# Moving the activations by 64 and 256 bytes in a two-layer encoder's MLPs, with the gates' weights and the sums of x handled at other places

## The chip, the cores and the metric

The kernel runs on one core of one Trainium2 chip. The metric is device time in microseconds (us) for one execution; three runs of a kernel give a median. A profile is one more execution, taken by the hardware profiler. Engines are named as the profile names them: PE is TensorE (PEld its weight loads), DVE is VectorE, ACT is ScalarE, POOL is GpSimd, SP is SyncE, which only issues DMAs here.

## What is computed

Two layers on x of 512 rows by 1024 features, all float32: layer 0 mixes by stick-breaking attention, layer 1 by a gated linear recurrence (RG-LRU), and each is followed by an MLP of squared ReLU with 4096 inner features.

```python
for layer in range(2):
    h = rms_norm(x, norm_mix[layer])
    x = x + (stick_breaking_attention(h, ...) if layer == 0 else rglru_block(h, ...))
    h = rms_norm(x, norm_mlp[layer])
    u = relu(h @ w1[layer]);  x = x + (u * u) @ w2[layer]
return rms_norm(x, norm_final)

# rglru_block: proj = h @ w_in; gate = gelu(proj[:, :1024]); xc = conv4(proj[:, 1024:])
# r, i = sigmoid of two block-diagonal products of xc (16 blocks of 64x64: "the gates' weights")
# log_a = -8 r softplus(-lam); hs = scan(a, sqrt(1 - a^2) * i * xc); y = (hs * gate) @ w_o
```

## The kernel before

**Numbers in two halves.** Every float32 product is made of three matmuls in the type fp32r: an operand is split into a high half (a cast, on ACT) and a low half (value minus high half, on DVE), and high x high, low x high and high x low are added in PSUM. Activations lie feature by row: `xgh` and `xgl` are the halves of x times the norm's weight, 8 chunks of 128 features by 512 rows, 2048 bytes of a partition for each chunk. `bh` and `bl` are a second pair of the same size. Weights come as 512 KB blocks by DMA (`raw`, or `b`), are split into `wh` and `wl`, and are used once. So for each block ACT casts for about 1.05 us and DVE subtracts for about 1.2 us.

**Order.** PE's instructions stand as the code writes them. The other engines' are placed by a scheduler at build time, except where the code chains them (`Ordered`). Each engine runs its own list in order and waits on semaphores.

**The MLP.** The first quarter of the inner features ("the squares", `squared`, lines 222 to 224 in the profile) is 8 dense products of 24 matmuls with 512 columns of x as the moving operand and a 128x128 weight tile as the stationary one. After it, products of two by two blocks are made by a scheme with seven products instead of eight (`PRODUCTS`: P1 to P7), which works on halves of rows and of features. There are four "down" stages of 14 parts (`times`, line 1067: the moving operand is `wh` or `wl`, 512 columns; the stationary one is the activation in `bh`, `bl`, `sh`, `sl`), and three "up" stages between them of 14 units (`up`, line 972: the moving operand is an activation, 256 columns, 24 matmuls a unit). An up stage runs P1, P5, P6, P3, P7, P2, P4 twice. What each reads as the moving operand is in `xa`: P1, P2 and P4 read `xgh` and `xgl` alone; P7 reads `xgh` and, for the low half, `low`; P3 and P5 read `s41` and `low`; P6 reads `s2` (in `bh` and `bl`) and `low`. P1 and P7 read chunks 0 to 3, P2 and P4 chunks 4 to 7.

**Sums of x.** `s41`, `s2`, `s3` and `low` hold halves of sums of chunks k and k+4 of x (`sums_of_x`: two ACT scalings, four DVE sums; `halves_of_sums`: three casts and three subtractions). They are needed from the first up stage on. k = 0 and 1 are done in the squares, k = 2 and 3 in the first down stage, at its places 19 and 20, 24 and 25; `replace` at place 26 puts `s3` over part of `xgh`. Place 14 is the first part of that stage, 27 its last.

**The gated recurrence.** Its steps on ACT, DVE and POOL follow a string, `ORDER`: `R` fetches raw gates' weights for four chunks, `W` and `X` make their halves, `f`, `a`, `x` fetch and split a weight block (`z0` is a block of the gate, `c2` of the conv's input), `P` is a product on PE, `N`, `r` the norm, `G` the gates' matmuls. The string begins with

```python
R0 fz0 fz1 fc3 Pc2 fc4 W1 W0 X1 X0 az0 xz0 N fc5 Pz0 az1 r ac3 jc3 W2 ac4 xz1 n0 fz2 n1 Pz1 b0 b1
```

`gate_raw` takes a tile `graw` of its own and fetches it on SP's queue (line 1405). In the product c2, after four of its eight chunks, PE makes the norm's sum (line 1470), which needs the squares of all eight chunks added up in `ssq` (line 159).

**Places in memory.** What lies where in a partition follows from the order in which tiles are made. In the built program `xgh`, `xgl`, `bh`, `bl`, `sh`, `sl` and the weights' `raw`, `wh`, `wl` begin at multiples of 128 bytes; all tiles of the attention, `low`, and `s41` begin 64 bytes past one. Chunks, halves and slices are whole multiples of 512 bytes, so an operand's place within 128 bytes is that of its tile. Two more weight buffers in the recurrence (pool `wmore`) lie 64 bytes past.

Of the kernel before, what the change touches and what calls it, by code (L numbers as in the profile page):

```python
# [11 lines left out]
F32 = mybir.dt.float32  # L12
F32R = mybir.dt.float32r
# [4 lines left out]
P = 128  # L18
S = 512
D = 1024  # L20
C = D // P
DFF = 4096
H = 16
HD = 64
EPS = 1e-6
RG_C = 8.0
SCALE = HD ** -0.5
ASIDE = 16


START = [
# [15 lines left out]


ORDER = """
R0 fz0 fz1 fc3 Pc2 fc4 W1 W0 X1 X0 az0 xz0 N fc5 Pz0 az1 r ac3 jc3 W2 ac4 xz1 n0 fz2 n1 Pz1 b0 b1  # L50
t0 ac5 jc4 n2 h0 X2 b2 l0 fc6 az2 t2 G0 jz2 Pc3 t1 s0 W3 h2 X3 h1 z1 R4 fz3 ac6 l1 l2 G1 n3 xc6 G2
s1 z0 Pc4 xc5 b3 s2 m0 fc7 fz4 fz5 m2 t3 E0 az3 T0 jz3 d0 Pc5 h3 E1 n4 ac7 m1 l3 T1 az4 d1 b4 E2
T2 G3 n5 jz4 d2 Pz2 fz6 xc7 q2 q0 t4 fz7 q1 s3 k0 W4 Pc6 h4 m3 b5 fo0 l4 W6 z2 k1 E3 g2 Pz3 n6 T3
# [9 lines left out]
def hybrid_encoder(  # L63
# [23 lines left out]
    nc = tc.nc  # L87
    V, A, G, PE = nc.vector, nc.scalar, nc.gpsimd, nc.tensor
# [15 lines left out]
    def f(ap):  # L104
        return ap.bitcast(F32)
# [11 lines left out]
    make_identity(nc, ident)  # L117
    eps_t = const.tile([P, 1], F32, tag="eps", name="eps_t")
    V.memset(eps_t, EPS)
    ss = const.tile([P, S // P, 3], F32, tag="ss", name="ss")  # L120
    bias = const.tile([P, S // P], F32, tag="bias", name="bias")

    xgh = const.tile([P, C, S], F32R, tag="xgh", name="xgh")
    xgl = const.tile([P, C, S], F32R, tag="xgl", name="xgl")
    bh = const.tile([P, C, S], F32R, tag="bh", name="bh")
    bl = const.tile([P, C, S], F32R, tag="bl", name="bl")

# [16 lines left out]
    class Squares:  # L144


        def __init__(self):
            self.acc = work.tile([P, S], F32, tag="ssq", name="ssq", bufs=1)
            self.begun = False
# [132 lines left out]
    NB = S // P  # L282
# [10 lines left out]
    with ExitStack() as actx:  # L293
# [238 lines left out]
        class Spread:  # L532
# [6 lines left out]
            def __getitem__(self, at):  # L539
                k = at[1] - self.k0  # L540
                return self.tiles[k // 4][:, k % 4, :]
# [198 lines left out]
    def residual(srcs, gname, begun={}, ready={}):  # L740

        for c in range(C):
            add_x(c, begun[c][0] if c in begun else dense(srcs[c], bh, bl, halves=ready.get(c)))
            halves(gname, c, x[c])

    residual(w_so, "mlp0", so, so_next)


    NQ = DFF // D
    HS = S // 2  # L750
# [21 lines left out]
    class Mlp:  # L772
# [170 lines left out]
        def replace(self):  # L943

            for i, t in enumerate(self.s3):
                self.A.copy(xgh[:, 2 * i : 2 * i + 2, HS:], f(t).rearrange("p (k n) -> p k n", k=2))

        def slots_of(self, p):

# [154 lines left out]
        def run(self, first, between, end):  # L1104
# [13 lines left out]
            def place(i):  # L1118

                return (i + self.STEPS // 2) % self.STEPS  # L1120
# [71 lines left out]
            def leave(i):  # L1192
# [6 lines left out]
                if kind == "down":  # L1199
                    if p:  # L1200
                        for n in range(2):
                            self.collect(name, n, bank[n])
                    prepare(ahead)
                    if q4 == 0:

                        k = {19: 2, 20: 2, 24: 3, 25: 3}.get(place(i))
                        if k:
                            (self.sums_of_x if place(i) in (19, 24) else self.halves_of_sums)(k)
                        if place(i) == 26:
                            self.replace()  # L1210
                    return
                u, three = us[p], bank.rearrange("p (i n) -> p i n", i=2)
# [85 lines left out]
        def quarters(self, between, end):  # L1298
            for c in range(C - 1):
                self.squared(c)  # L1300
                p, i = c // 4, c % 4 // 2
                if c % 2:
                    self.split(p, i, slice(0, 3), slice(0, 3))
                    self.sums(p, i)
                    self.split(p, i, slice(0, 4), slice(3, 7))
                if c == 0:
                    units = self.from_down(0)
                    self.load(units, *self.FROM_UP)
                if c < 2:

                    for n in range(4 * c, 4 * c + 4):
                        self.sq.chunk(n, x[n], e=V)
                if c == C - 2:
                    self.rr = self.sq.inv_squares(self.bank())
                between(c)

                k = c - 4
                if k in (0, 1):
                    with tc.issue_after(self.squares.ins):
                        self.sums_of_x(k)  # L1320
                        self.halves_of_sums(k)
            self.run(units, between, end)
            self.blocks.close()

    with ExitStack() as mctx:
# [16 lines left out]
            last["low"] = halves("mix1", c, x[c])  # L1342

        def end(ws, xs):
            for i in range(2):
                for g in range(2):
                    mlp.times("P4", g, i, ws[g], xs[i], False)
                mlp.collect("P4", i, xs[i])
                if i == 0:
                    for c in range(4, C):  # L1350
                        feature(c, "zzoo"[c - 4])
                        squares.chunk(c, x[c], e=G)
# [36 lines left out]
    with ExitStack() as rctx:  # L1389
# [11 lines left out]
        graw = {}  # L1401

        def gate_raw(c0):
            t = rp1.tile([P, 4, 2, HD], F32, tag="graw", name="graw")
            nc.sync.dma_start(out=t, in_=w_gate[:, c0 : c0 + 4])
            for c in range(4):
                graw[c0 + c] = t[:, c]

# [177 lines left out]
        for k in range(C):  # L1586
            for c in range(4):
                ps, wh, wl = begun[c]
                three(ps, bh[:, k, :], bl[:, k, :], wh[:, k, :], wl[:, k, :], k == 0, k == C - 1)

    residual(w_ro, "mlp1", begun, {4: ws["o4"]})
    wctx.close()


    with ExitStack() as mctx:
# [24 lines left out]


        A.activation(mlp.c[0][:, 0, :1], eps_t, AF.Sqrt)

        EV, EA = Ordered(V), Ordered(A)

# [152 lines left out]
```

## Time and profile before

| | |
|---|---|
| median of 3 runs | 1040.48 us (1039.40 to 1040.63) |
| profiled execution | 1040.69 us, of which the span from first to last instruction is 1039.0 us |
| PE, PEld | busy 1028.2 us (99%), 900.5 us (87%) |
| DVE, ACT, POOL | busy 863.4 us (83%), 702.2 us (68%), 167.0 us (16%) |
| granted TensorE clock | 0.998 of full speed over the span |
| HBM | 137.41 MB read, 136 GB/s over the span |

How to read what follows: a line of the chain of waits has start, length, engine, tile, source line and count. Matmuls overlap each other in the records (a matmul's own time is longer than the distance to the next), so the pace of PE is read from the chain's lengths, which go from start to start, or from two starts in the timeline. In the timeline a bracket gives the idle time before an instruction and what ended it.

### The profile page before, as it was taken

Reading aid. Unit: us, or ns where it says so; the run is one execution under the profiler, and the core shown is the slowest. Engines: PE = TensorE matmul, PEld = TensorE weight load, DVE = VectorE, ACT = ScalarE, POOL = GpSimd, SP = SyncE. Lnnn points to the kernel's source line nnn. Section 1 sums busy time; section 2 is a strip of 40 time slices with the busy share of each in tenths; the row PEclk is TensorE's granted clock in tenths of the full one; section 3 lists DMA queues with packets and bytes.
Section 4 is the critical chain, followed back from the end, with each engine's and each line's share of the span. In section 5 each row is a group of like instructions: output and inputs, shape, how many; then the busy total and the mean of one; then the engine's idle time right before and its main releaser. Section 6 shows DMA issues by size and latency. Waiting matters only on the chain.

```text
span 1039.0 us, 15867 instructions
## 1 busy us (share of the span) xinstructions
PE 1028.2 (99%) x5868; PEld 900.5 (87%) x5868; DVE 863.4 (83%) x1152; ACT 702.2 (68%) x1082; POOL 167.0 (16%) x233
## 2 busy tenths in 40 slices
PE   9999999999999999999999999999999999999997
PEld 7888888888888988988988788888888988988986
DVE  7888787848788898898899799984789798898897
ACT  6777676826766773774775699964755773863866
POOL 0444344420010010010011111100000010010012
PEclk9999999999999999999999999999999999999999
DMA  7745454528546667667682484352436667667663
GB/s 233 218 119 144 121 147 102 163 88 300 136 82 188 189 136 205 167 139 205 163 212 80 115 198 120 97 221 86 98 74 175 168 151 195 169 146 195 156 128 108
DMA packets 52829, 159.41 MB, mean 153 GB/s; under 512 B 6673, under 2 KB 7953, under 8 KB 52753
## 3 DMA queue, kind: packets, MB, share of 16 engines
q1 hardware_dynamic: 41664, 119.87, 35.3%
q0 software_dynamic: 10368, 37.75, 21.9%
q8 instruction: 46, 0.75, 0.3%
q10 hardware_dynamic: 720, 0.79, 0.2%
q14 instruction: 31, 0.25, 0.1%
HBM read 137.41 MB, written 4.19 MB: 136 GB/s over the span
## 4 chain that ended last, share of the span: by engine, by line
PE 87%; DVE 7%; issue 2%; ACT 2%; DMA 1%; DVEq 0%; SPq 0%; ACTq 0%; POOL 0%; POOLq 0%
PE ps_t L1067 13%; PE ps_acc L972 8%; PE ps_z L972 7%; PE ps_acc L1067 7%; PE ps_acc L222 5%; PE ps_acc L223 5%; PE ps_acc L224 5%; PE ps_o L972 4%; PE ps_z L1067 3%; DVE wl L762 2%; PE ps_t L223 2%; PE ps_t L224 2%; PE ps_t L222 2%; PE ps_o L222 2%; PE ps_o L223 2%; PE ps_o L224 2%
## 5 line engine op out<-in xcount | busy, mean ns | idle before, releaser
L762 ACT CAST wh<-b 128x1024 fp32r<-128x1024 f32 x168 | 174.4, 1051 | 124.9 <-DVE b L762 77.4
L762 DVE TENSOR_TENSOR wl<-b,wh 128x1024 fp32r<-128x1024 f32 x168 | 203.7, 1220 | 48.1 <-ACT wh L762 47.8
L1049 POOL DMA_DIRECT2D b<-in_w_dn x40 | 35.0, 875 | 357.9 <-DVE b L762 202.0
L222 PE MATMUL ps_acc<-xgh,wh 128*128 128x512 f32 x192 | 78.5, 409 | 0.0
L217 DVE TENSOR_TENSOR wl<-raw,wh 128x512 fp32r<-128x512 f32 (+2 forms) x70 | 62.1, 912 | 15.9 <-ACT wh L215 15.8
L223 PE MATMUL ps_acc<-xgh,wl 128*128 128x512 f32 x192 | 75.2, 392 | 0.0
L224 PE MATMUL ps_acc<-xgl,wh 128*128 128x512 f32 x192 | 75.1, 391 | 0.0
L586 DVE TENSOR_TENSOR_SCAN scan<-keep,later 128x128 f32<-128x128 f32 (+1 forms) x64 | 59.4, 931 | 17.1 <-ACT keep L576 10.5
L762 ACT ACTIVATE u<-u 128x512 f32<-128x512 f32 x100 | 63.1, 632 | 6.0 <-DVE u L762 4.3
L215 ACT CAST wh<-raw 128x512 fp32r<-128x512 f32 (+2 forms) x70 | 50.6, 759 | 23.0 <-PE ps_acc L224 7.3
L590 POOL TENSOR_TENSOR w<-w,scan 128x128 f32<-128x128 f32 (+1 forms) x64 | 51.4, 805 | 56.3 <-DVE scan L586 53.3
L762 DVE TENSOR_TENSOR b<-b,b 128x1024 f32<-128x1024 f32 x48 | 58.7, 1223 | 1.3
L1049 POOL DMA_DIRECT2D b<-in_w_up x24 | 20.8, 868 | 239.7 <-DVE b L762 71.7
L762 DVE TENSOR_TENSOR u<-u 128x512 f32<-128x512 f32 (+1 forms) x92 | 54.9, 596 | 2.7 <-ACT u L762 1.1
L972 PE MATMUL ps_z<-xgh,wh 128*128 128x256 f32 x192 | 54.3, 283 | 0.0
L972 PE MATMUL ps_z<-xgh,wl 128*128 128x256 f32 x192 | 54.1, 282 | 0.0
L762 ACT CAST wh<-raw 128x1024 fp32r<-128x1024 f32 x46 | 48.0, 1047 | 9.1 <-PE ps_acc L1067 8.3
L972 PE MATMUL ps_acc<-low,wh 128*128 128x256 f32 x192 | 53.5, 279 | 0.0
L1067 PE MATMUL ps_t<-wl,sh 128*128 128x512 f32 x126 | 49.2, 390 | 0.3 <-DVE wl L762 0.3
L1067 PE MATMUL ps_t<-wh,bh 128*128 128x512 f32 x126 | 49.2, 390 | 0.0
L1067 PE MATMUL ps_t<-wl,bh 128*128 128x512 f32 x126 | 49.1, 390 | 0.0
L1067 PE MATMUL ps_t<-wh,sl 128*128 128x512 f32 x126 | 49.1, 389 | 0.0
(398 smaller groups left out, 3416.0 us busy)
## 6 DMA issues: line engine op xcount, KB each, us to landing
b<-in_w_dn SPq DMA_DIRECT2D x48, 512.0 KB, 4.6
b<-in_w_dn POOLq DMA_DIRECT2D x40, 512.0 KB, 5.7
b<-in_w_up SPq DMA_DIRECT2D x36, 512.0 KB, 4.6
b<-in_w_up POOLq DMA_DIRECT2D x24, 512.0 KB, 5.5
raw<-in_w_m SPq DMA_DIRECT2D x16, 512.0 KB, 4.2
raw<-in_w_dn SPq DMA_DIRECT2D x16, 512.0 KB, 4.6
raw<-in_w_in SPq DMA_DIRECT2D x16, 512.0 KB, 4.3
raw<-in_w_qk SPq DMA_DIRECT2D x12, 512.0 KB, 3.8
```

The lines of the kernel that those rows point to most:

```text
L215: A.copy(wh[:, k, :], raw[:, k, :])
L217: V.tensor_tensor(wl[:, k, :], raw[:, k, :], f(wh[:, k, :]), ALU.subtract)
L222: PE.matmul(ps, wh, ah, start=start, stop=False)
L223: PE.matmul(ps, wl, ah, start=False, stop=False)
L224: PE.matmul(ps, wh, al, start=False, stop=stop)
L586: V.tensor_tensor_scan(sc[:, S - n : S][:, ::-1], keep[:, :n][:, ::-1], later[:, S - n :][:, ::-1], 1.0, ALU.mult, ALU.max,)
L590: G.tensor_tensor(wt, wt, sc[:, S - n + 1 : S + 1], ALU.mult)
L762: ins = getattr(self.e, name)(*args, **kwargs)
L972: PE.matmul(ps[:, i * HS : (i + 1) * HS], m, y, start=new and i == k == n == 0, stop=i == 1 and k == C // 2 - 1 and n == 2, skip_group_che ...
L1049: G.dma_start(out=unit[b].rearrange("p j n -> p (j n)"), in_=unit["src"](to), accum_op=ALU.add)
L1067: PE.matmul(ps, m, y[:, jj, cols], start=first and n == 0, stop=last and n == 2, skip_group_check=not new,)
```

## The change

Four things are edited.

- **Where x lies.** `xgh` and `xgl` become two views of one tile `x_t`, with 256 bytes (`FRONT`, 64 elements) left free ahead of the first and 512 ahead of the second. A call `x_down` sets how far down (towards lower addresses) the first chunk and the others lie: 256 and 64 bytes from each residual ahead of an MLP to the MLP's last products, and nothing elsewhere. `replace` now copies chunk by chunk (four copies of 128x256 for two of twice the size), since a view gives one chunk at a time.
- **Gates' weights.** `graw` takes the work pool's tile `sq` and is fetched on POOL's queue; in `ORDER` the splitting of z0 and z1 stands ahead of the gates' weights.
- **Sums of x.** In layer 1, k = 2 is done in the squares as well, k = 3 at places 19 and 20, and `replace` at place 21. Layer 0 keeps its places.
- **Small tiles.** `ss` and `bias`, used at the very end, move into columns of `colt` that are free by then.

```diff
-ASIDE = 16
+ASIDE, FRONT = 16, 64
 ORDER = """
-R0 fz0 fz1 fc3 Pc2 fc4 W1 W0 X1 X0 az0 xz0 N fc5 Pz0 az1 r ac3 jc3 W2 ac4 xz1 n0 fz2 n1 Pz1 b0 b1
+R0 fz0 fz1 fc3 Pc2 fc4 az0 xz0 az1 xz1 W1 W0 X1 X0 N fc5 Pz0 r ac3 jc3 W2 ac4 n0 fz2 n1 Pz1 b0 b1
...
-    ss = const.tile([P, S // P, 3], F32, tag="ss", name="ss")
-    bias = const.tile([P, S // P], F32, tag="bias", name="bias")
-    xgh = const.tile([P, C, S], F32R, tag="xgh", name="xgh")
-    xgl = const.tile([P, C, S], F32R, tag="xgl", name="xgl")
+    x_t = const.tile([P, 2 * C * S + 3 * FRONT], F32R, tag="xg", name="xg")
+    class Chunks:
+        def __init__(self, i):
+            self.start, self.down = FRONT + i * (C * S + 2 * FRONT), (0, 0)
+        def __getitem__(self, at):
+            p, c, cols = at
+            a = self.start + c * S - self.down[c > 0]
+            return x_t[p, a : a + S][:, cols]
+    xgh, xgl = Chunks(0), Chunks(1)
+    def x_down(*down):
+        xgh.down = xgl.down = down
...
+    x_down(FRONT, ASIDE)
     residual(w_so, "mlp0", so, so_next)
...
-                self.A.copy(xgh[:, 2 * i : 2 * i + 2, HS:], f(t).rearrange("p (k n) -> p k n", k=2))
+                for j in range(2):
+                    self.A.copy(xgh[:, 2 * i + j, HS:], f(t)[:, j * HS : (j + 1) * HS])
...
-                        k = {19: 2, 20: 2, 24: 3, 25: 3}.get(place(i))
+                        k = ({19: 2, 20: 2, 24: 3, 25: 3}, {19: 3, 20: 3})[self.layer].get(place(i))
...
-                        if place(i) == 26:
+                        if place(i) == 26 - 5 * self.layer:
                             self.replace()
...
-                if k in (0, 1):
+                if k in range(2 + self.layer):
...
         def end(ws, xs):
+            x_down(0, 0)
...
-            t = rp1.tile([P, 4, 2, HD], F32, tag="graw", name="graw")
-            nc.sync.dma_start(out=t, in_=w_gate[:, c0 : c0 + 4])
+            t = work.tile([P, S], F32, tag="sq", name="graw")
+            t = t.rearrange("p (c i n) -> p c i n", c=4, i=2)
+            G.dma_start(out=t, in_=w_gate[:, c0 : c0 + 4])
...
+    x_down(FRONT, ASIDE)
     residual(w_ro, "mlp1", begun, {4: ws["o4"]})
...
+        free = colt[:, COLS["conv"][0] :]
+        ss = free[:, : 3 * NB].rearrange("p (t i) -> p t i", i=3)
+        bias = free[:, 3 * NB : 4 * NB]
```

**Places after.** With `ss` and `bias` gone and 768 bytes added, every later tile moves by 672 bytes. Weights, `bh`, `bl`, `sh` and `sl` now begin 32 bytes past a multiple of 128, and the attention's tiles, `low` and `s41` begin 96 past. x lies 32 past outside the MLPs; in them its first chunk lies 32 past and the others 96 past. So the distances within 128 bytes between any two operands are what they were, but for chunks 1 to 7 of x in the MLPs. PE's list is the same instructions in the same order.

**DVE at the start of the recurrence, before**, from the last subtraction for `xgl` on (`wl` on line 217 is block c2, the two on line 762 are z0 and z1; line numbers in the second piece are those of the changed kernel, 14 to 15 higher here):

```order
L133 SCALAR_TENSOR_TENSOR xgl<-x,colt,xgh 128x512 x3
L217 TENSOR_TENSOR wl<-raw,wh 128x1024
L159 TENSOR_TENSOR ssq<-ssq,sq 128x512 x4
L762 TENSOR_TENSOR gl<-graw,gh 64x2x64 x4
L762 TENSOR_TENSOR wl<-raw,wh 128x1024
L762 RECIPROCAL r<-r 128x512
L762 TENSOR_TENSOR wl<-raw,wh 128x1024
L762 TENSOR_TENSOR ps_acc<-ps_acc,r 128x512 x2
```

and in the changed kernel:

```order
L147 SCALAR_TENSOR_TENSOR xg<-x,colt,xg 128x512 x3
L231 TENSOR_TENSOR wl<-raw,wh 128x1024
L173 TENSOR_TENSOR ssq<-ssq,sq 128x512
L777 TENSOR_TENSOR wl<-raw,wh 128x1024 x2
L173 TENSOR_TENSOR ssq<-ssq,sq 128x512 x3
L777 TENSOR_TENSOR gl<-graw,gh 64x2x64 x4
L777 RECIPROCAL r<-r 128x512
L777 TENSOR_TENSOR ps_acc<-ps_acc,r 128x512 x2
```

z0's and z1's low halves moved ahead of the gates' weights and of three of the four additions to `ssq`. ACT's casts for z0 and z1 moved in the same way, in among the last castings of x.

**DVE at the end of layer 1's squares, before**, from the reciprocal of the row norms on (`u` and `x` with 256 columns are sums of inner activations and of x):

```order
L176 RECIPROCAL rr<-rr 128x4
L762 TENSOR_TENSOR low<-x,s_7350 128x512
L762 TENSOR_TENSOR u<-u 128x256
L177 TENSOR_SCALAR rr<-rr 128x4
L762 TENSOR_TENSOR u<-u 128x256 x2
L762 TENSOR_TENSOR sl<-u,sh 128x1024
L762 TENSOR_TENSOR sl<-u,sh 128x768
L762 TENSOR_TENSOR wl<-b_7421,wh 128x1024
```

and in the changed kernel, from the second of the four sums for k = 2 on:

```order
L777 TENSOR_TENSOR x<-x 128x256
L777 TENSOR_TENSOR u<-u 128x256
L777 TENSOR_TENSOR x<-x 128x256
L777 TENSOR_TENSOR low<-x,s_7735 128x256
L777 TENSOR_TENSOR x<-x 128x256
L777 TENSOR_TENSOR sl<-u,sh 128x1024
L777 TENSOR_TENSOR low<-x,bl 128x256
L777 TENSOR_TENSOR low<-x,s_7349 128x512
L777 TENSOR_TENSOR sl<-u,sh 128x768
L777 TENSOR_TENSOR wl<-b_7420,wh 128x1024
```

The four sums and three subtractions for k = 2 moved here, ahead of `sl` and of the first `wl` of the down stage, from the middle of that stage.

## The prediction

> **What bounds the kernel now.** I read the page first: span, busy times, and the shares of the chain that ended last.
>
> ```profile
> span 1039.0 us, 15867 instructions
> PE 1028.2 (99%) x5868; PEld 900.5 (87%) x5868; DVE 863.4 (83%) x1152; ACT 702.2 (68%) x1082; POOL 167.0 (16%) x233
> PE 87%; DVE 7%; issue 2%; ACT 2%; DMA 1%; DVEq 0%; SPq 0%; ACTq 0%; POOL 0%; POOLq 0%
> ```
>
> PE is the bound. So there are two ways to gain: the pace of its matmuls, and the few places where it waits. The waits of PE, by who ended them:
>
> ```profile
> PE ps_t L223 <- DVE wl L762: 0.8, 1, 0.8
> PE ps_z L972 <- ACT u L762: 0.6, 1, 0.6
> PE ps_acc L972 <- ACT u L762: 0.4, 1, 0.4
> PE ps_t L1067 <- DVE wl L762: 0.3, 1, 0.3
> ```
>
> These four are what the edits outside the addresses can touch: the first stands at the start of the recurrence, the others in layer 1's first stages. For the pace I read the chain in time order through the second half of an up stage of layer 0. Its rows are P1, P5, P6, P3, P7, P2, P4 in this order, 24 matmuls each. The last row is 24 matmuls of a down stage, with 512 columns.
>
> ```profile
> 349.41 2.88 PE ps_z L972 x24
> 352.29 2.74 PE ps_o L972 x24
> 355.03 2.83 PE ps_z L972 x24
> 357.85 2.72 PE ps_o L972 x24
> 360.57 2.83 PE ps_z L972 x24
> 363.40 2.86 PE ps_o L972 x24
> 366.26 2.88 PE ps_z L972 x24
> ...
> 310.64 5.44 PE ps_acc L1067 x24
> ```
>
> The same 24 instructions of the same size take 2.72 us in P3 (113.3 ns each) and 2.88 us in P4 (120 ns). What differs is where the moving operand lies. P3 and P5 read `s41` and `low`, 64 bytes past a multiple of 128, while the weights begin at such a multiple. P1, P2 and P4 read x, which lies at the same place within 128 bytes as the weights. P6 and P7 read one tile of either kind, and take 2.83. So with 256 columns, operands at distance 64 go at 113.3 ns and operands at distance 0 at 120. I take this as a rule of this trace, since it holds in all seven products.
>
> The Trainium skill says otherwise (SBUF — State Buffer, the section on its two separate sides): PE has its own ports and never waits on another engine there, and weight loads have a second, independent read port; by that the place would not matter. The rows above disagree, 2.72 against 2.88 us, so I follow them.
>
> **Term A, the up stages.** The change puts chunks 1 to 7 of x at distance 64, as `s41` is now. Per unit of seven: P1 goes from 2.88 to 2.72, P2 from 2.86, P4 from 2.88, P7 from 2.83, and P5 loses the 0.02 in which it recovers from P1: 0.16 + 0.14 + 0.16 + 0.11 + 0.02 = 0.59 us. P6 reads `s2`, which doesn't move. But the first chunk lies at distance 0 still, in 6 of P1's 24 matmuls and in 4 of P7's. At 6.7 ns each that is 0.04 and 0.03, and each return from it costs about the 0.02 seen in P5, twice in P1 and perhaps once in P7. I take 0.12 off and use 0.47. There are 2 such halves in each of 3 stages in 2 layers, so 12 x 0.47 = 5.6 us. The best is 12 x 0.59 = 7.1; if the first chunk spoils P1 and P7 whole, P2, P4 and 0.02 are left, 12 x 0.32 = 3.8.
>
> **Term B, the squares.** These read x with 512 columns, and there the trace doesn't show distance 64 of this sign. At distance 0 a matmul takes 5.44 / 24 = 226.7 ns. The nearest row with distance 64, of the other sign (weights of pool `wmore` 64 past, x at 0), is product z1, whose first matmul and first successor are
>
> ```profile
> 589.73 0.39 PE L222 MATMUL ps_o<-xgh,wh 128*128 128x512 f32 x1
> 595.22 0.39 PE L1519 MATMUL ps_z<-bh,gh 128*128 128x512 f32 x1
> ```
>
> so 24 take 5.49 us, 228.8 ns each: with 512 columns distance 64 is the worse place, by 2.1 ns. Of each product of the squares 21 matmuls change; 16 products x 21 x 2.1 ns = 0.7 us, and I take a loss of 0.8. It might be nothing, or the full 6.7 ns of the narrow matmuls, 2.25 us.
>
> **Term C, the start of the recurrence.** The rows of SP's queue, ACT, DVE and PE:
>
> ```profile
> SPq L1405 <- DVE ssq L159: 2.3, 1, 2.3
> 576.90 0.33 SPq L1405 DMA_DIRECT2D graw<-in_w_gate  x1
> 580.75 1.26 ACT L762 CAST gh<-graw 64x128 fp32r<-64x128 f32 x4 [8.13 <-DMA graw<-in_w_gate]
> 582.04 1.05 ACT L762 CAST wh<-raw 128x1024 fp32r<-128x1024 f32 x1
> 573.94 2.94 DVE L159 TENSOR_TENSOR ssq<-ssq,sq 128x512 f32<-128x512 f32 x4
> 583.12 1.23 DVE L762 TENSOR_TENSOR wl<-raw,wh 128x1024 fp32r<-128x1024 f32 x1 [0.75 <-ACT wh L762]
> 579.40 1.02 PE L1470 MATMUL ps_z<-ssq,ones 128*128 128x512 f32 x2
> 582.79 0.39 PE L224 MATMUL ps_t<-xgl,wh 128*128 128x512 f32 x1
> 584.41 0.50 PE L223 MATMUL ps_t<-xgh,wl 128*128 128x512 f32 x1 [0.76 <-DVE wl L762]
> ```
>
> The gates' weights are fetched late, since their tile is free only after `ssq`; ACT idles 8.13 us for them, and z0's cast and subtraction stand behind. PE's second matmul of z0 was due two paces after 582.79, at 583.25, and started at 584.41, 1.16 late; with the restart I count 1.2 us. After the change z0 and z1 are split first: that wait goes. What is late next is the norm's sum on PE (L1470), which needs `ssq` complete. DVE begins these additions at 573.94 now and ends at 576.88; with two subtractions of about 1.2 us put in among them it ends near 579.3, and PE wants it at 579.40. ACT's two casts of 1.05 us also come in among the last castings of x, and may hold DVE up by as much as 1 us. So the new wait is 0 to 0.9 us; I take 0.4, and the gain is 0.8, with bounds of 0.3 and 1.2. Nothing else hides behind it: PE's order is the same, and the gates' own weights, now on POOL's queue and no longer behind `ssq`, are wanted only after z0 and z1 (first gates' matmul at 595.22).
>
> **Term D, the sums of x in layer 1.** Layer 0 and layer 1 run the same PE list here. I compare their first two down and up stages, start to start:
>
> ```profile
> 291.23 2.72 PE ps_t L1067 x12
> 446.71 2.75 PE ps_t L1067 x12
> ...
> 758.36 0.39 PE L1067 MATMUL ps_t<-wh,bh 128*128 128x512 f32 x1
> 916.87 2.75 PE ps_t L1067 x12
> ```
>
> Layer 0 takes 155.48 us and layer 1 takes 158.51: 3.0 us are lost to the waits listed above and to the restarts after them. They come late in the first down stage's work of DVE: there ACT waits for DVE (`wh` of `b`), and POOL's next DMA for DVE's `wl`. What one pair of chunks costs DVE is half of these rows, taken over the stretch with k = 2 and k = 3 (776 to 803 us):
>
> ```profile
> L762 DVE TENSOR_TENSOR x<-x 128x256 f32<-128x256 f32 x8 | 3.4, 423 | 0.2
> L762 DVE TENSOR_TENSOR low<-x,s 128x512 fp32r<-128x512 f32 x2 | 1.4, 692 | 0.2
> L762 DVE TENSOR_TENSOR low<-x,bl 128x256 fp32r<-128x256 f32 x2 | 0.8, 418 | 0.0
> L762 DVE TENSOR_TENSOR low<-x,s 128x256 fp32r<-128x256 f32 x2 | 0.8, 418 | 0.0
> ```
>
> (3.4 + 1.4 + 0.8 + 0.8) / 2 = 3.2 us leave the stretch ahead of the waits and go to the end of the squares, where DVE idles:
>
> ```profile
> 757.19 1.23 DVE L762 TENSOR_TENSOR sl<-u,sh 128x1024 fp32r<-128x1024 f32 x1 [1.11 <-ACT sh L762]
> 760.72 0.96 DVE L762 TENSOR_TENSOR sl<-u,sh 128x768 fp32r<-128x768 f32 x1 [2.31 <-ACT sh L762]
> 766.93 0.50 PE L1067 MATMUL ps_z<-wl,bh 128*128 128x512 f32 x1
> ```
>
> 1.11 + 2.31 = 3.4 us of idle time takes nearly all of it, but not quite: 2.1 us stand ahead of the first `sl` and delay the sums of u that ACT's `sh` waits for. By the rows the second `sl` comes 0 to 0.9 us later, and PE, which waits a little for DVE at 766.93 already, waits as much more. I take 0.65. So DVE is 3.2 - 0.65 = 2.5 us ahead where PE used to wait, and this stretch ends 2.5 us earlier: not 3.0 plus the two halves of term A in it, since DVE becomes the limit again. As 2 x 0.47 = 0.94 stand in term A, D is 1.6. It could be 2.0 with all 3.2 us gained, or -0.9 if DVE's work is only late at another place and PE can't use A's part there either.
>
> **Edits at no cost.** `replace` in four copies is ACT work and ACT is busy 68%; if its cover fails it is 0.4 us. `ss` and `bias` in `colt` leave ACT's and DVE's last instructions as they were.
>
> **The sum.** 5.6 - 0.8 + 0.8 + 1.6 = 7.2 us off the profiled execution's 1040.69 gives 1033.5. That execution lies 0.21 above the median of the runs, so against the runs it is 1033.3; I give 1033.4. Two runs of this kernel can be told apart from about 0.2%, 2 us.
>
> **The rivals.**
>
> *Everything works.* All terms at their best: 7.1 + 0 + 1.2 + 2.0 = 10.3 us, 1030.4. It needs the first chunk to cost nothing, for which no row speaks. Chance 0.15.
>
> *The squares pay and DVE is only late elsewhere.* B at 2.25, D at -0.9: 5.6 - 2.25 + 0.8 - 0.9 = 3.2, 1037.5. For it speaks that from 760.72 on DVE shows no idle time; against it, the 3.4 us of idle time just ahead. Chance 0.15.
>
> *The place doesn't matter.* If the difference between the products came from something else in them, A and B are 0, C is 0.8 and D its full 2.5: 3.3 us, 1037.4. By the Trainium skill's page named above (SBUF — State Buffer) this is what one would forecast. P1 to P7 have the same instruction and the same weights' buffers, and split exactly by tile, so I give it 0.06.
>
> *Slower: the shift of everything by 32 bytes.* All operands of PE lay at multiples of 64 bytes and now lie 32 past one. If such a start costs a matmul what distance 64 costs with 512 columns, 2.1 ns, then 5868 x 2.1 ns = 12.3 us are lost, and A and B vanish: 1040.7 + 12.3 - 3.3 = 1049.7. It decides from 7.2 us / 5868 = 1.2 ns a matmul on. One moving operand of the attention lies so now, `lastl`, beside `tl`, which lies at 64:
>
> ```profile
> L635 PE MATMUL ps_o<-lastl,v 128*128 128x256 f32 x16 | 4.6, 287 | 0.0
> L635 PE MATMUL ps_o<-tl,v 128*128 128x256 f32 x16 | 4.5, 282 | 0.0
> ```
>
> 287 against 282 ns in the records' own lengths: little speaks for it, but weights at such a place are not shown at all. Chance 0.12.
>
> **Chances and range.** The forecast itself, 1031.5 to 1035.5, has 0.52. The range 1030.3 to 1037.6 takes in the bounds of the terms and all cases but the slower one. Faster by more than 0.2%: 0.52 + 0.15 + 0.15 + 0.06, less a little for mixtures, 0.86; slower 0.12; within 0.2% 0.02.
>
> **What would show it.** In the changed profile's chain, rows of 24 at P2 and P4 with 2.72 (term A right) or 2.86 to 2.88 (wrong), P1 and P7 near 2.78; the squares' products of 24 near 5.49; no wait of PE for z0's `wl`, and perhaps one ahead of the norm's sum; layer 1's first two down and up stages in about 154 us. The prediction is wrong if P3 and P5 leave 2.72 or down-stage rows leave 5.44, which is the shift by 32 bytes; if P2 and P4 stay; or if PE waits more than 2 us in layer 1's first down stage.

## The result, and the profile after

The changed kernel takes 1037.43 us (median; 1036.74 to 1038.42), the kernel before, on the same chip, 1040.51 us. The ratio is 0.9973, with a 95% interval of 0.9962 to 0.9983. So it is faster, but by 3.1 us where 7.1 were forecast. The profiled execution took 1038.42 us.

The page of the changed kernel: span, busy times and the chain that ended last.

```profile
span 1036.7 us, 15868 instructions
PE 1026.0 (99%) x5868; PEld 893.5 (86%) x5868; DVE 861.0 (83%) x1152; ACT 702.5 (68%) x1086; POOL 174.2 (17%) x235
PE 78%; DVE 12%; ACT 6%; issue 3%; DMA 1%; SPq 0%; DVEq 0%; ACTq 0%
```

Before, 87% of the chain was PE and 7% DVE. Now DVE and ACT hold 18% of it together: in some stretches PE is no longer what ends last. The waits of PE say where (lines have moved: `down` is now L1083, `up` L988, the dense products L236 to L238, the helper L777):

```profile
PE ps_acc L443 <- ACT xg L146: 1.4, 2, 1.0
PE ps_t L1083 <- DVE wl L777: 1.2, 5, 0.3
PE ps_z L399 <- DVE eps_t L119: 1.1, 1, 1.1
PE ps_o L236 <- DVE x L752: 0.2, 1, 0.2
```

The waits at z0 and in layer 1's first stages are gone. New are five waits in the down stages, one behind an up stage each. The profile puts only 1.2 us on them, but they cost more: at the first one it lists 0.26 us, but against the kernel before PE loses 0.55 us there, and 0.35 us more a little earlier in the same stage, in small delays where no wait is listed. In the chain by order of time, the end of the first up stage and the down stage behind it:

```profile
345.26 2.72 PE ps_z L988 x24
347.98 2.72 PE ps_acc L988 x24
350.70 2.76 PE ps_z L988 x24
353.46 2.72 PE ps_o L988 x24
...
382.24 1.32 DVE c L777 x2
383.56 1.14 DVE b L777
...
384.78 1.06 ACT wh L777
...
385.87 1.24 DVE wl L777
...
387.15 2.79 PE ps_t L1083 x11
389.94 5.44 PE ps_acc L1083 x24
```

The first four rows are P2, P4, P1 and P5: 2.72, 2.72, 2.76 and 2.72, where 2.86, 2.88, 2.88 and 2.74 stood before. Then the chain leaves PE: a sum of weights on DVE (`b`), its cast on ACT, its subtraction on DVE, and PE starts 0.04 us after that.

To see what each stage gained or lost I lined up the starts of PE's matmuls, one by one, in both traces (negative is earlier than before):

| stretch | change, us |
|---|---|
| first 17 us | +0.9 |
| squares, layer 0 and layer 1 | +1.15, +1.0 |
| up stages, each of six | -0.93 |
| down stages behind the three up stages of layer 0 | +0.9, +0.65, +0.65 |
| down stages behind layer 1's second and third | +0.6, +0.35 |
| start of the recurrence | -0.9 |
| layer 1's first two down and up stages, with their two up stages | -3.7 |

The last row holds two of the six up stages, so 1.86 of its 3.7 us are theirs. The 0.9 us at the start I do not put down to the change: in the runs below the same stretch comes out between 0.55 us earlier and 1.6 later than before, and in the two that differ from the changed kernel only in sums made hundreds of microseconds later (the runs with three sums left out and with one sum by transfer) it comes out 0.4 and 0.15 us earlier.

### The profile page after: what moved, and what is told of

It is laid out like the page before. It is cut to its first block, busy times and chain, and to the rows that moved or that the text cites. A ratio compares the mean times of both kernels' runs of the same rounds, so it can differ in the third digit from the quotient of the medians.

```text
span 1036.7 us, 15868 instructions
## 1 busy us (share of the span) xinstructions
PE 1026.0 (99%) x5868; PEld 893.5 (86%) x5868; DVE 861.0 (83%) x1152; ACT 702.5 (68%) x1086; POOL 174.2 (17%) x235
## 4 chain that ended last, share of the span: by engine, by line
PE 78%; DVE 12%; ACT 6%; issue 3%; DMA 1%; SPq 0%; DVEq 0%; ACTq 0%
PE ps_t L1083 12%; PE ps_acc L988 8%; PE ps_acc L1083 6%; PE ps_acc L236 5%; PE ps_acc L238 5%; PE ps_acc L237 5%; DVE wl L777 4%; PE ps_z L988 3%; PE ps_z L1083 3%; DVE u L777 2%; PE ps_t L236 2%; PE ps_t L237 2%; PE ps_t L238 2%; ACT u L777 2%; ACT wh L777 2%
## 5 line engine op out<-in xcount | busy, mean ns | idle before, releaser
L777 ACT CAST wh<-b 128x1024 fp32r<-128x1024 f32 x168 | 174.5, 1050 | 122.3 <-DVE b L777 79.2
L777 DVE TENSOR_TENSOR wl<-b,wh 128x1024 fp32r<-128x1024 f32 x168 | 203.5, 1219 | 48.1 <-ACT wh L777 47.7
L236 PE MATMUL ps_acc<-xg,wh 128*128 128x512 f32 x192 | 78.7, 410 | 0.0
L238 PE MATMUL ps_acc<-xg,wh 128*128 128x512 f32 x192 | 75.3, 392 | 0.0
L237 PE MATMUL ps_acc<-xg,wl 128*128 128x512 f32 x192 | 75.3, 392 | 0.0
L777 ACT ACTIVATE u<-u 128x512 f32<-128x512 f32 x100 | 63.1, 632 | 7.8 <-DVE u L777 6.2
L988 PE MATMUL ps_z<-xg,wh 128*128 128x256 f32 x336 | 65.5, 277 | 0.0
L777 DVE TENSOR_TENSOR b<-b,b 128x1024 f32<-128x1024 f32 x48 | 58.7, 1223 | 1.3
L777 DVE TENSOR_TENSOR u<-u 128x512 f32<-128x512 f32 (+1 forms) x92 | 54.8, 596 | 2.6 <-ACT u L777 1.1
L988 PEld LDWEIGHTS ps_z<-xg,wh 128*128 128x128 f32 x336 | 53.8, 188 | 0.0
L777 ACT CAST wh<-raw 128x1024 fp32r<-128x1024 f32 x46 | 48.0, 1046 | 8.3 <-PE ps_acc L1083 8.3
L988 PE MATMUL ps_acc<-low,wh 128*128 128x256 f32 x192 | 53.4, 278 | 0.0
L988 PE MATMUL ps_z<-xg,wl 128*128 128x256 f32 x192 | 53.1, 277 | 0.0
L1083 PE MATMUL ps_t<-wl,sh 128*128 128x512 f32 x126 | 49.7, 394 | 1.2 <-DVE wl L777 1.2
L1083 PE MATMUL ps_t<-wh,bh 128*128 128x512 f32 x126 | 49.1, 390 | 0.0
L1083 PE MATMUL ps_t<-wh,sl 128*128 128x512 f32 x126 | 49.1, 390 | 0.0
```

The source lines that it names most:

```text
L236: PE.matmul(ps, wh, ah, start=start, stop=False)
L237: PE.matmul(ps, wl, ah, start=False, stop=False)
L238: PE.matmul(ps, wh, al, start=False, stop=stop)
L777: ins = getattr(self.e, name)(*args, **kwargs)
L988: PE.matmul(ps[:, i * HS : (i + 1) * HS], m, y, start=new and i == k == n == 0, stop=i == 1 and k == C // 2 - 1 and n == 2, skip_group_che ...
L1083: PE.matmul(ps, m, y[:, jj, cols], start=first and n == 0, stop=last and n == 2, skip_group_check=not new,)
```

## Experiments

**The places alone.** The kernel before's order of the gates' weights, `graw` and sums of x, with the changed kernel's places of x:

```
-R0 fz0 fz1 fc3 Pc2 fc4 az0 xz0 az1 xz1 W1 W0 X1 X0 N fc5 Pz0 r ac3 jc3 W2 ac4 n0 fz2 n1 Pz1 b0 b1
+R0 fz0 fz1 fc3 Pc2 fc4 W1 W0 X1 X0 az0 xz0 N fc5 Pz0 az1 r ac3 jc3 W2 ac4 xz1 n0 fz2 n1 Pz1 b0 b1
...
-                        k = ({19: 2, 20: 2, 24: 3, 25: 3}, {19: 3, 20: 3})[self.layer].get(place(i))
+                        k = {19: 2, 20: 2, 24: 3, 25: 3}.get(place(i))
...
-                if k in range(2 + self.layer):
+                if k in (0, 1):
...
-            G.dma_start(out=t, in_=w_gate[:, c0 : c0 + 4])
+            nc.sync.dma_start(out=t, in_=w_gate[:, c0 : c0 + 4])
```

> Only the places of x change; the recurrence's start, the order of the gates' weights and the sums of x stay as before. Theory 1 (handed back): the up stages gain 0.93 us a pair as forecast, 5.6 in all, but PE then reaches the next down stage earlier than DVE's last wl, so about 3 us are given back there; layer 1's first stages, where DVE is late anyway, give their 0.94 back whole; squares cost 2.2. That makes 5.6 - 2.2 - 3.2 - 0.9, within 1 us of the kernel before (1039.5 to 1041). Rival (the waits at the down stages come from the edits outside the places, as moved sums and splits): PE waits for no wl after the up stages, and the time is 5.6 - 2.2 = 3.4 us below before, 1037. Startup: if the 0.9 us that PE loses in the first 17 us is made by the places, it stands here too.

Measured: 1041.1 us, ratio 1.0005 (0.9996 to 1.0014): nothing. Each up stage but layer 1's first gains its 0.93 us, the squares lose 2.2 in all, and the five down stages hand 3.1 back. Layer 1's first two down and up stages, where DVE is late as before, gain 1.0 in place of the two up stages' 1.86. PE's largest wait:

```profile
PE ps_t L1083 <- DVE wl L777: 1.2, 5, 0.3
```

It is the changed kernel's row again, with neither the sums of x nor the gates moved. So the waits come from the places, that is, from PE's earlier arrival. The start of this run lies 0.5 us before the kernel before's.

**All but the places.**

```
-        xgh.down = xgl.down = down
+        xgh.down = xgl.down = (0, 0)
```

> All edits but the places: x has distance 0 from the weights in every stage, and everything still starts 32 bytes further. Theory 1: the up stages keep 2.86 to 2.88 for P1, P2, P4, the squares 5.44, no wait for wl after the up stages of layer 0; only the recurrence's start (0.9 us) and layer 1's first stages (1.6 to 2.5 us) gain: 1037.1 to 1038.0. Rival (start of every operand 32 bytes past a multiple of 64 costs something at the down stages): waits or a slower pace in the down stages of layer 0, and 1039 or more. If the 0.9 us at the startup comes from the places it is gone here; if it stands, it comes from another edit.

Measured: 1037.5 us, ratio 0.9974 (0.9963 to 0.9985), as much as the whole change. The start of the recurrence gains 0.95 us here; layer 1's first two down and up stages take 156.1 us, 2.2 less than before in the same count of matmuls. No down stage of layer 0 loses anything, with every operand 32 bytes further than before. So all that the changed kernel gains, two of its four edits give alone.

**All chunks of x 64 bytes down.**

```
-    x_down(FRONT, ASIDE)
+    x_down(ASIDE, ASIDE)
```

> The first chunk of x lies 64 bytes down as well, so P1 runs at 2.72 in place of 2.77 and P7 at 2.78 in place of 2.79: 0.8 us more off the up stages in all; the squares' three matmuls of the first chunk also go from 227 to 233 ns, 0.3 us more. Theory 1 (DVE sets the start of each down stage): the 0.8 us are handed back in longer waits for wl at the down stages, and the time is 0.2 to 0.5 us above the changed kernel. Rival (PE's pace sets the time throughout): 0.5 us below it.

Measured: 1039.9 us, ratio 0.9997 (0.9988 to 1.0006), 2.5 us above the changed kernel. Neither theory said that. The chain through the first up stage:

```profile
332.95 14.13 PE ps_acc L988 x120
347.08 2.83 PE ps_z L988 x24
...
355.56 2.83 PE ps_o L988 x24
```

Every product takes 2.83 us, P3 and P5 too, whose operands did not move and which took 2.72 before. Chunks 1 to 7 lie exactly as in the changed kernel. So "distance 64 goes at 113.3 ns" was wrong as a rule: at that distance the stream holds one of two paces, 113.3 or 117.8 ns. Something ahead must bring it into the quick one, and the first chunk at distance 0 does that in the changed kernel.

P7 of the changed kernel shows the switching from one matmul to the next. It takes each of chunks 0 to 3 by a group of three matmuls, two that read `xg` and one that reads `low`, and goes through the four chunks twice. In the group of chunk 0 the two lie at distance 0 and the third at 64; in the other groups all three lie at 64. The rows are the first matmul of chunk 1, of chunk 0 for the second time, of chunk 2 for the second time, and of P2:

```profile
342.65 0.28 PE L988 MATMUL ps_acc<-xg,wh 128*128 128x256 f32 x1
...
343.71 0.28 PE L988 MATMUL ps_acc<-xg,wh 128*128 128x256 f32 x1
...
344.42 0.28 PE L988 MATMUL ps_acc<-xg,wh 128*128 128x256 f32 x1
...
345.10 0.28 PE L988 MATMUL ps_z<-xg,wh 128*128 128x256 f32 x1
```

P3 ahead of it went at 113.3 ns a matmul. Behind the first group of chunk 0 nine matmuls take 1.06 us, 117.8 each; behind the second, once the pace has settled, six take 0.68 us, 113.3 each. The same three matmuls made the stream slow once and quick once. P6 consists of eight such groups (`s2` at 0, `low` at 64), and P3 behind it has the pace that P5 had ahead of it: the quick one in the changed kernel, the slow one in this run. So a few matmuls at distance 0 among others do not as such bring the quick pace. In the changed kernel's P1, where all three of chunk 0's group lie at distance 0, the pace behind it is the quick one each time. What sets the one or the other these runs don't settle.

**The last chunk at distance 0 in place of the first**, which tests the two paces by their order in time:

```
-        a = self.start + c * S - self.down[c > 0]
+        a = self.start + c * S - self.down[c == C - 1]
-    x_down(FRONT, ASIDE)
+    x_down(ASIDE, 0)
```

> Chunks 0 to 6 of x lie 64 bytes down, and the last chunk is the one at distance 0. Theory P (at distance 64 the stream of 256-column matmuls holds one of two paces, 113.3 or 117.8 ns, and matmuls at distance 0 ahead of it put it into the quick one; down stages with 512 columns leave it in the slow one): only P2 and P4 read the last chunk, at the end of their sums, so in the first half of each up stage P1, P5, P3 and P7 take 2.82 to 2.83 us as with all chunks at 64, and in the second half, after P2 and P4, P1, P5 and P3 take 2.72. The time is 0.3 to 2 us above the changed kernel. Rival 1 (distance alone sets the pace, and having all chunks at 64 was slow for another reason): P1, P5, P3 at 2.72 in both halves. Rival 2 (the first chunk itself, 256 bytes further down, is what the quick pace needs): 2.82 to 2.83 in both halves.

Measured: 1039.0 us, ratio 0.9988 (0.9979 to 0.9997). The chain through an up stage, from its first product to its last:

```profile
954.31 14.13 PE ps_acc L988 x120
968.45 2.80 PE ps_z L988 x24
971.24 2.76 PE ps_acc L988 x24
974.00 2.73 PE ps_z L988 x24
976.74 2.72 PE ps_o L988 x24
979.46 2.83 PE ps_z L988 x24
982.28 2.72 PE ps_o L988 x24
985.00 2.72 PE ps_z L988 x24
```

Five products of the first half take 14.13 / 5 = 2.83 us each. P2, in which the last chunk first comes, takes 2.80, and in the second half the same five take 2.73, 2.72, 2.83, 2.72 and 2.72. That is Theory P to the row; both rivals fall. Five of the six up stages run so. In layer 1's first one PE is held up by 0.16 us at the change from P3 to P7 in the second half, near 829 us. Behind that P7 goes at 117.8 ns, with every operand where it lies in the other five stages, and P2's last chunk brings the quick pace back. So the place alone doesn't fix the pace even there.

**Other distances: 32 and 128 bytes down.**

```
-    x_down(FRONT, ASIDE)
+    x_down(FRONT, 8)      (32 bytes; the other run: 32, 128 bytes)
```

> Chunks 1 to 7 of x lie 32 bytes down instead of 64, the first chunk stays. If only the place within 128 bytes counts and any distance but 0 is alike: P2 and P4 at 2.72 and the squares at 233 ns, time as the changed kernel, 1037. If 32 bytes are too little to part the operands: P2 and P4 at 2.88 and the squares at 226.7, time as without the shift of x, 1037.5. If they part the narrow ones without harm to the wide ones: up stages 0.93 us a pair quicker and squares 226.7, and 2.2 us below the changed kernel, less what the down stages hand back.

> Chunks 1 to 7 of x lie 128 bytes down. If only the place within 128 bytes counts, this is distance 0 again: P1, P2 and P4 at 2.86 to 2.88, squares 226.7 ns, the time as without the shift of x, 1037 to 1038. If the distance counts as such, P2 and P4 leave 2.88.

Measured: 1038.7 us, ratio 0.9983 (0.9974 to 0.9992), at 32 bytes; 1037.7 (one run) at 128. From both chains P2 and P4, first at 32 bytes:

```profile
345.12 2.84 PE ps_z L988 x24
347.96 2.84 PE ps_acc L988 x24
```

and at 128 bytes:

```profile
344.15 2.84 PE ps_z L988 x24
347.00 2.85 PE ps_acc L988 x24
```

Neither is 2.72, and 128 is not quite 0 either, though it is the same place within 128 bytes. The squares show it better. With x 32 bytes down a product takes 5.59 us, so none of the three cases expected there came, and with x 128 bytes down it still takes 5.59, as at 64:

```profile
257.22 0.39 PE L236 MATMUL ps_t<-xg,wh 128*128 128x512 f32 x1
262.81 0.39 PE L236 MATMUL ps_t<-xg,wh 128*128 128x512 f32 x1
```

**64 bytes up.** The first chunk at the tile's start, the others 64 bytes above their old distance, smaller margins around x:

```
-    x_down(FRONT, ASIDE)
+    x_down(0, -ASIDE)
...
-            self.start, self.down = FRONT + i * (C * S + 2 * FRONT), (0, 0)
+            self.start, self.down = i * (C * S + 32), (0, 0)
```

> Chunks 1 to 7 of x lie 64 bytes up instead of down, the first chunk at distance 0 as before; the margins around x are 512 bytes smaller, so that everything behind x lies 512 bytes lower. If only the place within 128 bytes counts, the up stages' products and the squares' 233 ns are as in the changed kernel, and so is the time, 1037 to 1038. If the side counts, as the third product of the recurrence with weights 64 bytes past and x at the multiple gives 229 ns, the squares take 5.49 us per 24 matmuls in place of 5.58, and it is 1.4 us quicker, less what the down stages hand back.

Measured: 1040.0 us, ratio 0.9999 (0.999 to 1.0008). Here the first chunk does not bring the quick pace: P1 takes 2.81 or 2.82, the others 2.82 to 2.84. The squares take 5.53 us, between the two expected values. So more of the addresses counts than their place within 128 bytes; which part, these runs don't settle, the less so as this run also moves the first chunk and every tile behind x.

**Three of DVE's sums left out** (SUMS, the sums of inner activations that DVE makes at the end of an up stage; those operands then keep older sums):

```
-                            last_sums(u, self.SUMS[:2])
+                            last_sums(u, self.SUMS[:1])
-                    last_sums(u, self.SUMS[2:3])
-                    last_sums(u, self.SUMS[3:])
```

> The changed kernel without three of the four last sums of inner activations that DVE makes at the end of each up stage (left out, so those operands keep older sums): DVE has 3 x 0.7 = 2.1 us less to do ahead of the next down stage. Theory 1: PE's waits for wl behind each up stage vanish, and the 3.2 us handed back come home: 1034 to 1035. Rival (the waits come from ACT's chain of casts and squares, or from the weights' DMA): waits stay, within 0.7 us of the changed kernel.

Measured: 1033.7 us, ratio 0.9938 (0.9925 to 0.995), 3.7 us below the changed kernel. PE waits in no down stage; its two largest waits are

```profile
PE ps_z L399 <- DVE eps_t L119: 1.1, 1, 1.1
PE ps_o L649 <- DVE tl L638: 0.8, 1, 0.8
```

and both stand outside the MLPs. Lined up as in the table above, the five down stages hand back nothing (0.01 us at most). So the gain of the up stages was there all along, and DVE's chain took it back.

**The same three sums on POOL** (`G` in the code).

```
...
+                    last_sums(u, self.SUMS[1:], G)
```

> The three sums that the run without them left out are made, but on POOL, which is busy 17%. Theory 1 (DVE's work at the end of an up stage sets the start of the next down stage): DVE has the same 2.1 us less to do, PE's waits for wl go, and the time is 1034 to 1035, unless POOL needs so long for the sums that the split of their results comes late. If POOL takes over 4 us for the three, PE waits for that split instead, or POOL's own DMA issues behind the sums come late: then 1037 or more.

Measured: 1047.7 us, ratio 1.0071 (1.0057 to 1.0085). Slower than before, and PE waits for DVE's `wl` more than ever. PE's largest wait:

```profile
PE ps_acc L1083 <- DVE wl L777: 5.4, 6, 0.9
```

POOL's three sums in the timeline of the same down stage as above, and two instructions of DVE beside them:

```profile
375.63 5.22 POOL L1184 TENSOR_TENSOR u<-u 128x512 f32<-128x512 f32 x3 [0.27 <-DVE u L777]
```

```profile
375.79 2.22 DVE L777 TENSOR_TENSOR wl<-raw,wh 128x1024 fp32r<-128x1024 f32 x1 [0.25 <-ACT wh L777]
377.93 1.77 DVE L777 TENSOR_TENSOR sl<-u,sh 128x512 fp32r<-128x512 f32 x1
```

The same two take 1.22 and 0.69 us in the changed kernel. While POOL adds, these two of DVE's two-operand instructions become 1.0 and 1.1 us longer, and the two `wl` behind them take 3.45 us for 2.35. So DVE lost 3.2 us here where it was spared 2.1. POOL's three sums took 5.2 us, more than the 4 us named in the expectation, but PE waits for `wl`, as theory 1 has it, and not for the split. The Trainium skill (SBUF — State Buffer, the section on its two separate sides) says that a DVE instruction with two SBUF inputs and a GpSimd one that reads SBUF exclude each other for a whole instruction; these rows agree.

**One sum later, and three sums later, on DVE.** The last sum goes to just ahead of its split at place 22 of the down stage, or three sums to their splits at places 20 and 22:

```
+                    if waiting and place(i) == 22:
+                        last_sums(us[1], self.SUMS[3:])
-                    last_sums(u, self.SUMS[3:])
```

> The changed kernel with the last of the four sums of inner activations made later by DVE: not at the end of the up stage, but just ahead of its own split in the down stage, behind the wl that PE waits for. DVE does the same work in all. Theory 1: the wl come 0.6 us earlier in each of the five down stages behind an up stage, where PE waited 0.35 to 0.9 us: about 2.6 us less, 1034.5 to 1035.5. Rival (DVE has no room anywhere, so work moved back makes PE wait further on in the down stage): waits for sl or wl behind that place, 1037 to 1038.

> As with the last sum later, but three of the sums stand just ahead of the splits that read them in the down stage: 1.3 us more leaves DVE's stretch ahead of the wl, and the split of u's first part waits for two of them. Theory 1: waits for wl as good as gone, 1034 to 1035, unless that split comes late for PE; then PE waits for sl and it is slower than with one sum moved.

Measured: 1039.5 us, ratio 0.9995 (0.9986 to 1.0003), and 1045.3, ratio 1.0055 (1.0043 to 1.0067). With one sum later the wait at 387 us is gone, and one a little further on has its place:

```profile
388.66 1.82 PE ps_acc L1083 x9
...
390.51 1.24 DVE wl L777
```

That stage now hands back 0.55 us where it handed back 0.9, and the next three 0.5 to 0.6 where they handed back 0.6 to 0.65. The program's last down stage, whose parts come in another order, loses 2.5 us against 0.35. The late sum delays an `sl` there. Then DVE falls 1.1 us behind and stays so to the end, for another reason: two subtractions that take 2.35 us together in the changed kernel take 3.45, the second of them while POOL makes a two-operand sum of its own. In the changed kernel:

```profile
1015.21 2.35 DVE L777 TENSOR_TENSOR wl<-b,wh 128x1024 fp32r<-128x1024 f32 x2
```

and in this run:

```profile
1015.23 3.45 DVE L777 TENSOR_TENSOR wl<-b,wh 128x1024 fp32r<-128x1024 f32 x2
1016.21 1.39 POOL L1664 TENSOR_TENSOR c<-c,gb 128x512 f32<-128x512 f32 x1 [6.32 <-ACT junk L777]
```

So the picture is the rival's, that DVE has little room and work moved back moves the wait; of the 1.5 us above its 1038, 1.1 come from the meeting with POOL at the end. With three sums later PE waits 5.1 us for `wl` in twelve waits, and not for the `sl` that was named.

**One sum later, x not shifted.**

> The last sum later as well, but x not shifted in any stage. Theory 1: PE is not early at the down stages, so DVE's relief has nothing to give: within 0.5 us of the run without shift, 1037 to 1038. Rival (the postponed sum is a gain by itself): 2 us or more below that run.

Measured: 1039.45 us, ratio 0.9996 (0.9987 to 1.0004): 2 us above the run without shift, 1.7 of them in that same last down stage, where DVE and POOL meet again (a `wl` of 2.32 us for 1.22). Up to there the postponed sum costs nothing and gives 0.4 us, in layer 1's second down stage.

**One sum by an accumulating transfer**, which takes work off DVE without POOL's arithmetic:

```
-                    last_sums(u, self.SUMS[3:])
+                    G.dma_start(
+                        out=u[1].rearrange("p i n -> p (i n)"),
+                        in_=u[0].rearrange("p i n -> p (i n)"), accum_op=ALU.add,
+                    )
```

> The changed kernel with the last of the four sums (u's second part += its first) made by an accumulating DMA from POOL's queue in place of DVE. Theory 1, in the form that DVE's amount of work between the up stage's end and the middle of the down stage is what PE waits for: 0.6 us less of it behind each of the five up stages that are followed by a wait, 0.35 to 0.65 handed back there, so 2 to 3 us come home: 1034.5 to 1035.5. Rivals: the transfer lands too late for the split of u's second part, or POOL's next weights' transfer comes late behind it, and PE waits for sl or wl there: 1037 or more; or the transfer slows DVE as POOL's own sums did, and nothing is gained.

> The same transfer in place of DVE's last sum, with x not shifted. Theory 1: PE arrives late enough at the down stages without the shift, nothing waits there, so the relief gives nothing: within 0.6 us of the run without shift, 1037 to 1038. Rival (less work for DVE is a gain by itself): 2 us below it.

Measured: with x shifted 1034.34 us, ratio 0.9947 (0.9933 to 0.996); with x not shifted 1037.59, ratio 0.9974 (0.9965 to 0.9983). PE's waits in the first:

```profile
PE ps_z L399 <- DVE eps_t L119: 1.1, 1, 1.1
PE ps_o L236 <- DVE x L752: 0.2, 1, 0.2
```

Two by two this settles the cause:

| | sum on DVE | sum by transfer |
|---|---|---|
| x not shifted | 1037.5 | 1037.6 |
| x shifted | 1037.4 | 1034.3 |

The shift gives nothing alone, the transfer gives nothing alone (its trace shows 0.4 us, in layer 1's second down stage), and both together give 3.1 us. Lined up as in the table above, the five down stages hand back 0.2 us in all with the transfer, where the changed kernel's hand back 3.2, so the 3.1 us lie where the waits stood. PE must come early and DVE must be ready. This version is 3.1 us below the changed kernel and 6.0 below the one before.

## Why the prediction was wrong, point by point

**Term A, the up stages: right in size, wrong in what stood behind it.** P2 and P4 went to 2.72, P1 to 2.76 and 2.77, P7 to 2.79, P5 lost its 0.02; an up stage gained 0.93 us against 2 x 0.47. But the step "operands at distance 64 go at 113.3 ns", taken as a rule from seven products, does not hold: with all chunks there they go at 117.8. What I deducted as a flaw, the first chunk at distance 0, is what brought the quick pace, and P7's price was not a return from it but the slow pace over half of the product. That the size came out to 0.01 us a stage was luck.

**The step that failed: 12 x 0.47 = 5.6 us went into the sum as if PE alone set the end of each stage.** For layer 1's first stages I did ask what DVE would do if PE came earlier; for the five other down stages I did not. There DVE had next to nothing to spare in one and 0.3 to 0.6 us in the others: PE came 0.93 us early, and the table gives 0.9 + 0.65 + 0.65 + 0.6 + 0.35 = 3.2 us handed back. The kernel before hints at it in the busy times by stretch: from 366 to 388 us, around the start of that down stage, DVE is busy 20.56 of 22 us and PE 22.00.

```profile
366.00:388.00 22.00, 22.00 (x111) 18.74 (x110) 20.56 (x26) 15.63 (x21) 4.34 (x5) 1.00 0.67 124
```

(columns: length, then busy time and instructions of PE, weight loads, DVE, ACT and POOL; clock, DMA share, GB/s). No wait of PE stood there, and I read that as slack.

**Term B, the squares: mis-sized.** A loss of 0.8 us was taken, at 2.1 ns a matmul from z1; it is 2.15 us in all, at the bad end that was named. Over a product's 24 matmuls it is (5.59 - 5.44) / 24 = 6.3 ns. A product after the change, from its first matmul to the next one's:

```profile
264.00 0.39 PE L236 MATMUL ps_t<-xg,wh 128*128 128x512 f32 x1
269.59 0.39 PE L236 MATMUL ps_acc<-xg,wh 128*128 128x512 f32 x1
```

That is 5.59 us where 5.49 was forecast. z1 itself takes 5.49 still: the nearest row had the distance, but not the addresses.

**Term C, the start of the recurrence: right.** It gained 0.9 us against 0.8, with no wait for z0's `wl` left, and the norm's sum a little late as foreseen:

```profile
580.32 0.39 PE L238 MATMUL ps_t<-xg,wh 128*128 128x512 f32 x1
580.82 1.10 PE L1488 MATMUL ps_z<-ssq,ones 128*128 128x512 f32 x2
```

One pace after 580.32 is 580.55, so 0.27 us late.

**Term D, the sums of x in layer 1: right in size, wrong in its account.** By itself, without the shift, it is 2.2 us. In the changed kernel the stretch runs from

```profile
759.62 0.40 PE L1083 MATMUL ps_t<-wh,bh 128*128 128x512 f32 x1
914.28 0.39 PE L1083 MATMUL ps_t<-wh,bh 128*128 128x512 f32 x1
```

that is 154.7 us, where the same matmuls took 158.35 before. The "about 154" of the prediction doesn't follow from its own term: 2.5 us less gives about 156. The stretch holds two up stages, so 1.9 us of term A, not 0.94, and DVE did not become the limit in it again: of the 3.7 us gained 1.9 are A, whole, and 1.8 are D.

**The sum** with what was measured is -5.6 + 2.15 - 0.9 - 1.8 + 3.2 = -2.95 us; the medians lie 3.1 apart. (The two profiled spans lie 2.3 apart, with the 0.9 us at the start.) Of the 4.2 us between this and the forecast, 3.2 are the failed step, 1.35 the squares; C and D came out 0.3 better.

**The rivals.** The nearest one in time was the right picture in half: the squares pay their full price, and DVE is late elsewhere, 1037.5. But it put DVE's lateness into layer 1's first stages, where the moved sums did bring what was forecast, and not behind the other up stages. That its time is met so closely is luck. "The place doesn't matter" gave 1037.4 and is refuted: places change products from 2.72 to 2.88 us. The Trainium skill (SBUF — State Buffer, the section on its two separate sides) says that PE never waits on another engine there. That the place would not matter either was the prediction's own reading of it, and the rows of six placements disagree with that reading. The shift by 32 bytes cost nothing: down rows stay at 5.44, P3 and P5 at 2.72.

## What to carry to other kernels

When an engine with 99% busy time is made quicker in one stage, ask at the start of each next stage how far the second busiest engine is from being late there. "No wait" in the trace says it is in time now, not by how much. A wait can be removed by less work on the late engine, hardly by the same work at another time, and not by an engine that slows it. And a pace read off a few products of one program is a pace of that sequence: vary the place once before it is used as a rule.

## What the runs showed of the hardware

- A stream of 256-column matmuls with its moving operand 64 bytes beside the weights, within 128, has two steady paces, 113.3 and 117.8 ns: the slow one was held over 144 matmuls in a row with all chunks 64 bytes down, the quick one over some 55 in the changed kernel. A group of three in which the first two lie at distance 0 changed the pace either way (P7 of the changed kernel), a group with all three at 0 was followed by the quick one (P1), and a delay of 0.16 us was followed by the slow one (one P7 with the last chunk at 0). At distance 0 the pace is 120 ns (P4 before). With x 64 bytes up, no product reached the quick pace.
- With 512 columns it is 226.7 ns with x at its old place and 230 to 233 with x moved by 32, 64 or 128 bytes down or 64 up: the opposite sign, and no function of the place within 128 bytes alone. What sets it stays open.
- DVE's instructions with two operands take about 1.1 us longer each while POOL makes a two-operand sum: 2.22 for 1.22 and 1.77 for 0.69 with the sums on POOL, and 3.45 for 2.35 over two with the last sum later.
- An accumulating transfer of 128x512 took 3.3 to 5.6 us from issue to landing and 0.87 us of POOL, and spared DVE an instruction of 0.69 us.
